# Three 16-element vectors: loaded as rows and spread over the partitions by a matmul with ones, instead of loaded spread

## The chip, the cores and the metric

The kernel runs on one core of a Trainium2 chip. The metric is the device time of one execution in microseconds (us); the median of three runs of the kernel before is 1518.44 us (1517.57 to 1518.94). TensorE (PE) multiplies, VectorE (DVE) and ScalarE (ACT) work elementwise, GpSimd (POOL) does little here, and the sixteen DMA engines move data. SyncE (SP) issues nearly all transfers on one queue (q1 in the profile), POOL issues a few on another (q0), ACT two at the start (q10). All queues are served by the same sixteen DMA engines.

## What is computed

One decoder block over 1024 tokens of width 1024 in float32: RMSNorm, one input projection, a Mamba-2 mixer beside a retention mixer, an output projection, a SwiGLU feed-forward, a final RMSNorm. The change touches only how three vectors with one value for each of the 16 Mamba heads reach the chip:

```python
dt = jax.nn.softplus(dt_raw.astype(jnp.float32) + dt_bias.astype(jnp.float32))
a = -jnp.exp(a_log.astype(jnp.float32)).reshape(SSD_GROUPS, SSD_HPG)
a_cs = jnp.cumsum(dt_c * a, axis=2)
...
d = d_skip.astype(jnp.float32).reshape(SSD_GROUPS, SSD_HPG, 1)
y = y_diag + y_off + x_c.astype(jnp.float32) * d
```

`dt_bias`, `a_log` and `d_skip` are (1, 16) each, 64 bytes.

## The kernel before

Every float32 product is made from three matmuls: each operand is split into a rounded part and a remainder (ACT copies, line 248; DVE subtracts, line 249). The program is a list of steps. A block is one strip of up to 512 columns of a weight with 8 or more steps, usually one for each 128 rows of the weight; a step runs 12 matmuls of up to 512 columns. `advance` runs ahead of the steps: it issues the weight loads (`load`, line 238, on SP, into a ring of five buffers `wr`) and the splits (`divide`, lines 248 and 249). `at(i, f)` hangs other work behind step i.

The program's start is written by hand. SP's queue holds, in order: a tile of x (`x0`, 512 KB), four weight tiles of 256 KB (below: weight tiles 0 to 3), the next tile of x (`x1`, 512 KB), then weight tiles 4 to 7, and after them narrower weight tiles, `x2`, `x3` and the constants `kcB`. ACT's queue holds the identity (64 KB) and one small load. The first block, `v0`, keeps all its eight weight tiles, split, in `m0` to `m7`. Its 8 steps are run token tile by token tile: 12 matmuls with weight tiles 0 to 3 for token tile 0, then `x1` is transposed (`turn`, 8 transposes, line 163), 12 matmuls with weight tiles 4 to 7 for token tile 0, 12 with tiles 0 to 3 for token tile 1, and so on. `turn(t)` also has ACT (line 1177) and DVE (line 1178) scale the transposed tile and split it into `h0` to `h7`. ACT works strictly in the program's order, in which the splits of weight tiles 4 to 7 alternate with pieces of `h`.

The names that the change touches:
- `hb` (128 x 32) holds `dt_bias` and `-exp(a_log)`, the same on each of the 128 partitions. `dcol` (128 x 8) holds `d_skip`, the even heads on partitions 0 to 63 and the odd ones on 64 to 127. `hb` is first read by the step that makes dt (line 510, at 57.05 us), `dcol` by the Mamba output (line 664, from 206.3 us).
- `load_small`, called while the start is laid out, issues the loads of `kcB` (SP) and of `dcol` and `hb` (POOL). `partition_broadcast` makes a source that is read again for each partition; for `dcol` the source is also read with a stride of two elements.
- `use_small` and `make_cols(False)` are called together from `late_small`, which hangs behind step 12. `make_cols` transposes the other small vectors (`rows`) on PE and copies them to `cols` by ACT.
- `bank("M")` draws the next of three PSUM banks in turn; `mm` is a matmul kept in program order; `T(shape, "at")` draws the buffer named `at`, which the kernel uses again later.

Of the kernel before, what the change touches and what calls it, by code (L numbers as in the profile page):

```python
# [12 lines left out]
AF = mybir.ActivationFunctionType  # L13
# [4 lines left out]
P = 128  # L18
# [6 lines left out]
SH, SP_, SG = 16, 64, 2  # L25
# [40 lines left out]
def block_kernel(ctx: ExitStack, tc: tile.TileContext, x, norm1_w, w_in, conv_w, conv_b,  # L66
                 dt_bias, a_log, d_skip, ssd_norm_w, ret_norm_w, w_out, norm2_w, w_gate,
                 w_up, w_down, final_norm_w, consts, out):
    nc = tc.nc
# [9 lines left out]
    def T(shape, tag, dt=F32, bufs=1):  # L79
        uid[0] += 1  # L80
        return sb.tile(list(shape), dt, tag=tag, name=f"{tag}_{uid[0]}", bufs=bufs)

    def bank(tag):
        uid[0] += 1
        return psum.tile([P, 512], F32, tag=tag, name=f"{tag}_{uid[0]}", bufs={"L": 5, "M": 3}[tag])
# [5 lines left out]
    act = nc.scalar.activation  # L91
# [17 lines left out]
    hb = T([P, 2 * SH], "hb")  # L109
    dcol = T([P, 8], "dcol")  # L110
    ones = T([P, P], "ones")
    nc.vector.memset(ones, 1.0)

    def use_small():
        act(hb[:, SH:2 * SH], hb[:, SH:2 * SH], AF.Exp)
        ts(hb[:, SH:2 * SH], hb[:, SH:2 * SH], -1.0, None, op0=ALU.mult)

    def load_small():
        nc.sync.dma_start(kc, consts[:, P:])
        for j in range(2):  # L120
            nc.gpsimd.dma_start(dcol[64 * j:64 * j + 64, :],
                                d_skip[0].rearrange("(k j) -> j k", j=2)[j]
                                .partition_broadcast(64))
        for j, src in enumerate((dt_bias, a_log)):
            nc.gpsimd.dma_start(hb[:, j * SH:(j + 1) * SH], src[0].partition_broadcast(P))

    dtb = hb[:, 0:SH]
    aneg = hb[:, SH:2 * SH]
# [30 lines left out]
    def mm(o, a, b, start=True, stop=True, **kw):  # L159
        tc.keep_in_program_order(nc.tensor.matmul(o, a, b, start=start, stop=stop, **kw))  # L160
# [1024 lines left out]
    b = bank("M")  # L1185
# [10 lines left out]
    for t in (2, 3):  # L1196
        first_load(t)
    load_small()
    at(ROWS, first_rows)

    def late_small():

        with tc.issue_after(newest["act"]), tc.issue_after(newest["dve"]):
            use_small()
            make_cols(False)
# [78 lines left out]
```

## Time and profile before

| | |
|---|---|
| median of the runs | 1518.44 us |
| the profiled execution | 1518.63 us |
| its span in the trace | 1516.8 us |
| PE busy | 1493.7 us (98%) |
| DVE busy | 1015.4 us (67%) |
| ACT busy | 630.4 us (42%) |
| granted PE clock, mean | 0.995 |

The chain of waits goes back from the last instruction to what released it, step by step; PE has 95% of the span in it and DMA 3%. Granted clock 1.00 is 2.4 GHz, 0.50 is 1.2 GHz. In a timeline each row is start and length in us, engine, line, operation, what is written and read, count, and in brackets the idle time before it with what ended it. In the table of stretches each row has, for each engine, busy us and count of instructions, then the granted clock (PEclk), the DMA engines' mean busy share (1.00 is all sixteen busy) and GB/s. In a table of DMA queues each row has packets, MB and the time the packets took as a share of sixteen engines' time.

### The profile page before, as it was taken

How to read it: one execution, taken by the hardware profiler on the slowest of the kernel's cores; microseconds unless marked ns; L12 is line 12 of the kernel's file. 1: busy time of each engine (PE TensorE's matmuls, PEld its weight loads, DVE VectorE, ACT ScalarE, POOL GpSimd, SP SyncE). 2: the span in 40 equal slices, each digit the busy share in tenths (PEclk: the TensorE clock that was granted, in tenths of full speed). 3: DMA queues.
4: the chain of work that ended last, by engine and by line, in shares of the span. 5: the costliest groups of instructions: out<-in, count | busy, mean ns of one | idle time of the engine just before them, and what ended most of it. 6: DMA issues, size and time to landing. Idle time of an engine off the chain costs nothing.

```text
span 1516.8 us, 20817 instructions
## 1 busy us (share of the span) xinstructions
PE 1493.7 (98%) x7408; PEld 1222.5 (81%) x7408; DVE 1015.4 (67%) x2171; ACT 630.4 (42%) x1223; POOL 35.9 (2%) x67
## 2 busy tenths in 40 slices
PE   7999999999999999999999999999999999999997
PEld 5888878888789878878888788888888887888886
DVE  4587698767688896579645977666666666346345
ACT  5344457444355665334544532233323334334231
POOL 1011000000001000000000000000000000000000
PEclk8999999999999999999999999999999999999999
DMA  7433466463425558645534323222222328355331
GB/s 197 137 92 98 113 208 187 126 236 111 133 71 152 165 181 268 222 140 175 190 116 131 111 82 107 84 77 84 84 82 79 97 96 309 116 187 182 125 118 63
DMA packets 141481, 209.73 MB, mean 138 GB/s; under 512 B 11236, under 2 KB 71488, under 8 KB 141376
## 3 DMA queue, kind: packets, MB, share of 16 engines
q1 hardware_dynamic: 140208, 206.95, 43.7%
q0 software_dynamic: 432, 0.59, 0.6%
q8 instruction: 58, 0.95, 0.3%
q10 hardware_dynamic: 736, 0.86, 0.2%
q14 instruction: 47, 0.39, 0.1%
HBM read 167.39 MB, written 40.96 MB: 137 GB/s over the span
## 4 chain that ended last, share of the span: by engine, by line
PE 95%; DMA 3%; ACT 1%; DVE 1%; issue 0%; SPq 0%; ACTq 0%
PE L L160 76%; PE M L160 17%; PE M L163 2%; DMA m<-aD 1%; DMA wr<-in_w_in_dram 1%; DMA wr<-in_w_down_dram 0%; DMA qk<-aD 0%; DMA kc<-in_consts_dram 0%; ACT m L195 0%; SPq L1058 0%; DVE wp L249 0%; ACT x L449 0%; DVE m L196 0%; ACT wp L248 0%; DVE u L1020 0%
## 5 line engine op out<-in xcount | busy, mean ns | idle before, releaser
L249 DVE TENSOR_TENSOR wp<-wr,wp 128x512 fp32r<-128x512 f32 (+2 forms) x328 | 218.2, 666 | 226.6 <-ACT wp L248 223.6
L160 PE MATMUL L<-wp,m 128*128 128x512 f32 x1512 | 356.1, 395 | 0.5 <-DVE wp L249 0.3
L248 ACT ACTIVATE wp<-wr 128x512 fp32r<-128x512 f32 (+2 forms) x328 | 199.7, 609 | 361.2 <-PE L L160 303.2
L160 PEld LDWEIGHTS L<-wp,m 128*128 128x128 f32 x1512 | 282.3, 188 | 66.2 <-DVE wp L249 0.8
L160 PE MATMUL L<-h,wp 128*128 128x512 f32 x1104 | 266.5, 397 | 0.0
L160 PE MATMUL L<-wp,h 128*128 128x512 f32 (+2 forms) x1248 | 260.0, 365 | 0.0
L160 PEld LDWEIGHTS L<-h,wp 128*128 128x128 f32 x1104 | 205.4, 188 | 49.5 <-issue 1.0
L160 PEld LDWEIGHTS L<-wp,h 128*128 128x128 f32 x1248 | 215.3, 188 | 30.6 <-issue 5.1
L160 PE MATMUL L<-m,x 128*128 128x512 f32 x336 | 82.3, 393 | 0.0
L160 PE MATMUL L<-m,wp 128*128 128x512 f32 x312 | 77.0, 395 | 0.0
L160 PEld LDWEIGHTS L<-m,x 128*128 128x128 f32 x336 | 63.0, 188 | 14.8
L160 PEld LDWEIGHTS L<-m,wp 128*128 128x128 f32 x312 | 58.5, 188 | 14.2
L392 DVE SCALAR_TENSOR_TENSOR m<-m,cols,m 128x512 f32<-128x512 f32 x72 | 52.1, 745 | 3.6 <-ACT m L390 3.4
L160 PE MATMUL M<-m,wp 128*128 128x512 f32 x216 | 53.5, 396 | 0.0
L160 PE MATMUL L<-h,x 128*128 128x512 f32 x204 | 50.6, 396 | 0.5 <-DVE wr L1018 0.5
L160 PEld LDWEIGHTS M<-m,wp 128*128 128x128 f32 x216 | 40.5, 188 | 10.1 <-DVE wp L196 0.3
L1011 ACT ACTIVATE wr<-wr 128x512 f32<-128x512 f32 x33 | 20.9, 632 | 66.0 <-DVE wr L1009 64.9
L160 PE MATMUL M<-m,x 128*128 128x512 f32 x192 | 47.1, 394 | 0.0
L160 PEld LDWEIGHTS L<-h,x 128*128 128x128 f32 x204 | 38.1, 188 | 10.0 <-DVE wr L1018 1.0
L195 ACT ACTIVATE x<-x 128x512 fp32r<-128x512 f32 x27 | 17.0, 629 | 64.5 <-PE L L160 43.6
L196 DVE TENSOR_TENSOR m<-m 128x512 fp32r<-128x512 f32 x32 | 21.9, 691 | 32.6 <-ACT m L195 32.3
L160 PEld LDWEIGHTS M<-m,x 128*128 128x128 f32 x192 | 36.0, 188 | 8.6
(294 smaller groups left out, 1981.6 us busy)
## 6 DMA issues: line engine op xcount, KB each, us to landing
wr<-in_w_in_dram SPq DMA_DIRECT2D x144, 256.0 KB, 2.7
wr<-in_w_down_dram SPq DMA_DIRECT2D x88, 256.0 KB, 2.9
wr<-in_w_out_dram SPq DMA_DIRECT2D x64, 256.0 KB, 3.0
aD<-u SPq DMA_DIRECT2D x44, 256.0 KB, 2.0
x<-in_w_gate_dram SPq DMA_DIRECT2D x22, 512.0 KB, 3.9
x<-in_w_up_dram SPq DMA_DIRECT2D x22, 512.0 KB, 4.6
x<-in_x_dram SPq DMA_DIRECT2D x16, 512.0 KB, 4.1
m<-rD SPq DMA_DIRECT2D x16, 512.0 KB, 4.2
```

Source lines behind the costliest of these rows:

```text
L160: tc.keep_in_program_order(nc.tensor.matmul(o, a, b, start=start, stop=stop, **kw))
L163: tc.keep_in_program_order(nc.tensor.transpose(o, a, ident))
L195: a = act(pair[:, 0], src, AF.Copy).ins
L196: d = tt(pair[:, 1], src, pair[:, 0].bitcast(F32), op=ALU.subtract).ins
L248: newest["act"] = act(pair[:, 0, :n], raw[:, :n], AF.Copy).ins
L249: newest["dve"] = tt(pair[:, 1, :n], raw[:, :n], pair[:, 0, :n].bitcast(F32), op=ALU.subtract).ins
L392: stt(dst, u[:, q:q + TH], w[q], dst, op0=ALU.mult, op1=ALU.add)
L1011: act(t, g, AF.Tanh, scale=0.5)
```

## The change

`load_small` now loads only `kcB`. Three loads of 16 elements each bring `dt_bias`, `a_log` and `d_skip` into one row `small` on one partition; they are issued on POOL's queue ahead of the memset of `halo`. `use_small` makes one matmul with a row of ones (one partition, 128 columns) as the stationary operand and `small` (one partition, 48 columns) as the moving one, which leaves the 48 values on all 128 partitions of a PSUM bank. From there ACT copies `dt_bias`, takes the exponential of `a_log`, and copies the even and odd elements of `d_skip` to the two halves of `dcol`; DVE negates as before.

```diff
+    small = T([1, 3 * SH], "at")
+    for j, src in enumerate((dt_bias, a_log, d_skip)):
+        nc.gpsimd.dma_start(small[:, j * SH:(j + 1) * SH], src)
+
     def use_small():
-        act(hb[:, SH:2 * SH], hb[:, SH:2 * SH], AF.Exp)
+
+        b = bank("M")
+        mm(b[:, :3 * SH], ones[:1, :], small)
+        act(hb[:, :SH], b[:, :SH], AF.Copy)
+        act(hb[:, SH:2 * SH], b[:, SH:2 * SH], AF.Exp)
         ts(hb[:, SH:2 * SH], hb[:, SH:2 * SH], -1.0, None, op0=ALU.mult)
+        d = b[:, 2 * SH:3 * SH].rearrange("p (k j) -> p j k", j=2)
+        for j in range(2):
+            act(dcol[64 * j:64 * j + 64, :], d[64 * j:64 * j + 64, j, :], AF.Copy)
 
     def load_small():
         nc.sync.dma_start(kc, consts[:, P:])
-        for j in range(2):
-            nc.gpsimd.dma_start(dcol[64 * j:64 * j + 64, :],
-                                d_skip[0].rearrange("(k j) -> j k", j=2)[j]
-                                .partition_broadcast(64))
-        for j, src in enumerate((dt_bias, a_log)):
-            nc.gpsimd.dma_start(hb[:, j * SH:(j + 1) * SH], src[0].partition_broadcast(P))
```

POOL's order at the program's start, before: two loads for `dcol` (64 partitions, 8 runs of one element each) and two for `hb` stand behind the memset.

```order
L105 DMA rows_66<-in_ssd_norm_w_dram 8x128
L140 MEMSET halo_79 128x36
L121 DMA dcol_75<-in_d_skip_dram 64x8x1 x2
L125 DMA hb_74<-in_dt_bias_dram 128x16
L125 DMA hb_74<-in_a_log_dram 128x16
```

And of the changed kernel at the same place:

```order
L105 DMA rows_66<-in_ssd_norm_w_dram 8x128
L116 DMA at_78<-in_dt_bias_dram 1x16x1
L116 DMA at_78<-in_a_log_dram 1x16x1
L116 DMA at_78<-in_d_skip_dram 1x16x1
L145 MEMSET halo_83 128x36
```

Four loads have become three; the elements written went from 1024 single ones and 256 runs of 16 to 48 single ones (the last number of a shape is the run).

ACT's order around step 12, before: the exponential stands between two splits of weight tiles (line 248), the copies to `cols` (line 137) behind them.

```order
L248 ACTIVATE wp_89_573<-wr_85_537 128x272
L115 ACTIVATE hb_5_74<-hb_5_74 128x16
L248 ACTIVATE wp_92_597<-wr_86_554 128x272
L137 ACTIVATE cols_8_78<-M_90_590 128x8
L137 ACTIVATE cols_8_78<-M_90_590 128x68
L137 ACTIVATE cols_8_78<-M_90_590 128x8
```

And of the changed kernel (line 253 is the split, line 142 the copies to `cols`):

```order
L253 ACTIVATE wp_90_573<-wr_85_537 128x272
L253 ACTIVATE wp_94_602<-wr_87_554 128x272
L122 ACTIVATE hb_5_74<-M_91_588 128x16
L123 ACTIVATE hb_5_74<-M_91_588 128x16
L127 ACTIVATE dcol_6_75<-M_91_588 64x8 x2
L142 ACTIVATE cols_9_82<-M_92_595 128x8
L142 ACTIVATE cols_9_82<-M_92_595 128x68
```

The one instruction has become four, which read PSUM and stand behind the split and directly ahead of the copies to `cols`.

## Rows read from the trace of the kernel before

**Rows 1.** Chain of waits, 0 to 60 us: start, length in us, what.
```profile
5.03 13.78 DMA wr<-in_w_in_dram
...
19.77 1.65 PE L L160 x3
21.42 1.71 PE M L163 x8
23.12 6.46 PE L L160 x24
29.58 0.87 PE M L163 x8
30.45 5.49 PE L L160 x24
...
52.59 0.07 PE M L135
```

**Rows 2.** Timeline of ACT, 5 to 28 us.
```profile
8.65 0.71 ACT L1177 ACTIVATE h<-M,cols 128x128 fp32r<-128x128 f32 x2
18.83 0.63 ACT L248 ACTIVATE m<-wr 128x512 fp32r<-128x512 f32 x1 [9.47 <-DMA wr<-in_w_in_dram]
...
19.62 0.62 ACT L248 ACTIVATE m<-wr 128x512 fp32r<-128x512 f32 x1
...
22.31 0.62 ACT L1177 ACTIVATE h<-M,cols 128x128 fp32r<-128x128 f32 x2 [0.51 <-PE M L163]
...
27.74 0.39 ACT L1177 ACTIVATE h<-M,cols 128x128 fp32r<-128x128 f32 x1
```

**Rows 3.** Stretches of the start: PE, PEld, DVE, ACT, POOL busy; PEclk, DMA share, GB/s.
```profile
0.00:8.00 8.00, 6.35 (x30) 5.33 (x30) 1.71 (x4) 3.48 (x7) 5.58 (x14) 1.00 0.80 264
8.00:15.00 7.00, 2.10 (x6) 0.97 (x6) 2.07 (x5) 1.36 (x4) 0.00 (x0) 0.99 1.10 48
...
10.40:19.80 9.40, 0.03 (x1) 0.03 (x1) 0.31 (x1) 0.97 (x3) 0.00 (x0) 0.74 0.79 137
19.80:25.00 5.20, 5.20 (x16) 4.33 (x17) 3.93 (x10) 4.46 (x14) 0.00 (x0) 0.50 0.90 315
```

**Rows 4.** DMA queues, 8 to 15 us: packets, MB, share of 16 engines.
```profile
q0 software_dynamic: 52, 0.01, 97.0%
q1 hardware_dynamic: 161, 0.33, 12.6%
```

**Rows 5.** DMA queues, 15 to 19 us, POOL's queue.
```profile
q0 software_dynamic: 80, 0.02, 2.0%
```

**Rows 6.** DMA issues: count, KB each, median us from issue to landing.
```profile
dcol<-in_d_skip_dram POOLq DMA_DIRECT2D x2, 2.0 KB, 11.5
rows<-in_conv_w_dram POOLq DMA_DIRECT2D x1, 24.0 KB, 4.7
...
hb<-in_dt_bias_dram POOLq DMA_DIRECT2D x1, 8.0 KB, 13.5
```

**Rows 7.** Timeline of the issues on SP and POOL, 0 to 30 us.
```profile
5.03 10.48 SPq L238 DMA_DIRECT2D wr<-in_w_in_dram  x5
...
5.51 0.59 POOL L125 DMA_DIRECT2D hb<-in_dt_bias_dram  x1
```

**Rows 8.** Timeline of ACT and PE, 50 to 56 us.
```profile
51.44 0.20 ACT L115 ACTIVATE hb<-hb 128x16 f32<-128x16 f32 x1
...
52.42 0.24 PE L135 MATMUL M<-kc,rows 84*128 84x84 f32 x1
...
52.62 0.43 ACT L248 ACTIVATE wp<-wr 128x272 fp32r<-128x272 f32 x1 [0.98 <-PE L L160]
52.96 0.34 ACT L137 ACTIVATE cols<-M 128x8 f32<-128x8 f32 x3
...
54.26 0.64 ACT L248 ACTIVATE wp<-wr 128x512 fp32r<-128x512 f32 x1 [0.95 <-PE L L160]
```

**Rows 9.** Groups of ACT by line: busy us, mean ns, idle before.
```profile
L137 ACT ACT_TABLE_LOAD x1 | 1.3, 1283 | 1.8 <-issue 1.8
```

## The prediction

> **What bounds the kernel now.** I read the chain of waits first. Nearly the whole span in it is PE, so a change counts if it shortens the time in which PE has nothing to do, or in which its clock is low. The largest such time is at the start: a load of a weight tile takes 13.78 us from its issue at 5.03 us and is followed by a split on ACT at 18.83, and only then does PE go on [rows 1, 2]. The timeline of ACT shows the same from its side: it ends a piece of h at 9.36 (8.65 + 0.71), then waits 9.47 us for a weight tile [rows 2]. This is weight tile 4, the fifth on SP's queue. The stretches show what this costs twice: from 10.4 to 19.8 PE has 0.03 us of work, the granted clock is 0.74 on average there, and from 19.8 to 25.0 it is 0.50, which is 1.2 GHz, while PE is busy all the time [rows 3].
>
> Next I asked what the DMA engines did meanwhile. Up to 8 us they moved 264 GB/s, from 8 to 15 us 48 GB/s, at a DMA share of 1.10 [rows 3]: busy, but moving nothing. The queues tell who held them: from 8 to 15 us POOL's queue has 52 packets and 0.01 MB at 97.0% of sixteen engines' time, SP's queue 0.33 MB at 12.6% [rows 4]. POOL's loads at that time are the two of dcol and the two of hb. The two of dcol are 2 KB each and land after 11.5 us in the median, against 4.7 us for the twelve times larger load of conv weights just ahead on the same queue [rows 6]. The loads of hb, 16 KB together, are issued from 5.51 us on and land 13.5 us later, about 19 us, and from 15 to 19 us POOL's queue moves 0.02 MB at only 2.0% [rows 5 to 7]. So it is dcol, not hb, that holds the engines: 97.0% of 16 engines for 7 us is 108.6 us of engine time for 1024 separate elements of four bytes, 0.106 us each. The hb packets, whose runs are 16 elements long, cost 1.3 us of engine time in all.
>
> The Trainium skill, DMA: Bandwidth & Descriptors, section Rules for kernel authors, says that a strided last dimension lowers to one descriptor for each element. The trace agrees, with 0.106 us for each element here.
>
> **The change part by part.** *The loads.* The four loads go, and with them the 108.6 us of engine time. Three loads come, each listed as 16 runs of one element, so they are still element by element: 48 elements instead of 1024. At 0.106 us each that is 5.1 us of engine time, 0.3 us if spread over sixteen engines. The bounds are nothing (the packets of hb, 80 of which with their neighbours took 1.3 us) and one whole dcol packet for each of the three loads on each engine; I take 0.3, because the number of elements is what the 97.0% follows. They follow the same five loads on POOL's queue as dcol's did, and nothing waits for them until step 12.
>
> The Trainium skill, same page, section Why a DMA increments its semaphore by 16, says that software can split a contiguous row so that it goes over sixteen engines; the listing's 1x16x1 fits. By this splitting the sum is 0.3 us; without it, with a row of 64 bytes as one run, it would be nothing.
>
> *When weight tile 4 comes now.* Ahead of its last byte on the queues are 0.11 MB of small things, x0 and x1 (1.05 MB) and five weight tiles (1.31 MB), 2.47 MB. By 8.0 us 2.11 MB had moved (264 GB/s by 8 us) [rows 3]. The other 0.36 MB takes 1.1 us at the 315 GB/s of the stretch from 19.8 to 25.0, 1.4 us at 264: it lands at 9.1 to 9.4, with the new elements at 9.4 to 9.7. ACT is free for it at 9.36. I take 9.6, so the split that started at 18.83 starts **9.2 us earlier**. Bounds: 9.47 (no wait at all) and 8.5: tiles 5 to 7 follow each other in 0.83 to 0.99 us (262 KB at those rates) where ACT takes one each 0.79 us (18.83 to 19.62) [rows 2], which can lose another 0.1 to 0.6. SP issued four of them late because the issues themselves were held, five issues in 10.48 us [rows 7]; with the engines free I expect them as soon as their buffers are.
>
> *The clock.* Up to the stall the granted clock is 1.00 with PE busy 6.35 of 8 us [rows 3]; it falls after PE had been idle for some microseconds, and without that idleness I expect it to stay at 2.4 GHz. Before, the way from 19.77 to 29.58 was 3 matmuls in 1.65, 8 transposes in 1.71 and 24 matmuls in 6.46 us, together 9.82 [rows 1]. At full clock 24 matmuls take 5.49 (0.229 each) and 8 transposes 0.87 [rows 1]; the same work is 27 x 0.229 + 0.87 = 7.05. That is 2.77 us less, if ACT and DVE keep up. What is late next is ACT: it evacuates token tile 1 without a gap from 22.31 to 28.13 [rows 2]. Without PE's slow transposes it begins this when the fourth split is done, 3.0 us after the first one starts (3 x 0.79 + 0.62) instead of 3.5. PE needs the fourth piece about 7.5 us after the first split, ACT and DVE give it some 0.3 us later than that. I take **2.4 us**, bounds 1.5 (ACT's squares of x get in the way further) and 2.77.
>
> *The tail of the shift.* After 30.45 the chain is PE without a break [rows 1], and the weight tiles and x2, x3 behind on SP's queue move forward with it, since they wait for buffers that are free earlier, or for the queue. I count the shift whole to the end.
>
> *Step 12.* PE gets one more small matmul, next to the transposition of the small vectors, which takes 0.24 us of PE's time and 0.07 on the chain [rows 1, 8]. Bounds 0.07 and 0.24, I take **0.1**. Its three loads are long done. ACT gets four small instructions where it had one of 0.20 us; like their neighbours they are 0.11 (three in 0.34) to 0.20 each, so 0.45 to 0.8 us, directly ahead of the copies to cols. Queued behind them are these copies and the split at 54.26. Before, ACT ended the copies at 53.30 and then waited 0.95 us for PE to free a split buffer [rows 8]: this wait hides them. Without that cover they would cost up to 0.8 us. Copies and exponentials alternate in both kernels, and the whole execution has one table load [rows 9], so none is added. DVE's negation comes one split later; hb is needed at 57 us, dcol at 206. One more draw of a PSUM bank makes each next draw wait for the one three draws back, which is long free there: nothing.
>
> **The sum**, against the profiled execution's own 1518.63 us, 0.2 above the median: - 9.2 - 2.4 + 0.1 = - 11.5, **1507.1 us**. With the bounds: - 9.47 - 2.77 + 0.07 gives 1506.5, - 8.5 - 1.5 + 0.24 gives 1508.9.
>
> **The rivals.** *Packets cost by their number, not by their elements, and the new loads are slower (slower than before).* The two loads of dcol, if each is one packet on each of sixteen engines, are 32 packets of 3.4 us (108.6 / 32). If a packet of one element were held as long, three loads would hold each engine 10.2 us instead of 6.8, and weight tile 4 would come 3.4 us later than now: 1522.0. It decides from 2.3 us for such a packet (6.8 / 3). For it: 1x16x1 is again one element at a time. Against it: 52 packets with 0.01 MB took 108.6 us, 80 with 0.02 MB 1.3 us [rows 4, 5], so it isn't the number.
>
> *They cost in between.* A short packet may be held for part of a latency. At the mean of the 52 packets, 2.1 us (108.6 / 52), three hold an engine 6.3 us, 6.0 more than in my sum: 1513.1; at 0.5 us each, 1.5 us, it is 1508.3. Middle of it: 1510.5. For it: nothing in the trace shows a one-element packet of data. Against: transfers ahead of them on the queue pass in 4.7 us with little engine time. The Trainium skill, DMA: Bandwidth & Descriptors, section Anatomy of one DMA, gives a fixed cost of about 2.0 us for each DMA, most of it the write's receipt; if that were engine time, this rival's upper end would be the result, an estimate of 1512.8 from that page.
>
> *The clock falls all the same*, because PE in this phase waits often in small pieces, so only the wait is won: 1518.63 - 9.2 + 0.1 = 1509.5. Against it: those small waits stood at clock 1.00 before 10 us.
>
> *The change doesn't do what it says*: something else, such as POOL's loads as such, holds the engines: 1518.7, no change. Against it: rows 5.
>
> **How the numbers follow.** A measurement of this kernel can tell about 0.2%, 3.0 us, from no change. My forecast of 1507.1 (1506.4 to 1508.9) has 0.78; in-between packets 0.10; the clock lost 0.05; no change 0.03; slower by packets 0.04. The first three are faster by over 0.2%: 0.93. The range holds my forecast with its bounds and the runs' own scatter (0.9 us), the lost clock and the nearer half of the in-between case: 1505.6 to 1510.4.
>
> **What would show it.** In the changed kernel's trace ACT's wait for a weight tile near 9.4 us should be under 0.5 us, POOL's queue should be under 5% of the engines' time from 8 to 15 us, PE's granted clock should be 1.00 throughout the first 30 us, and the 24 matmuls after the transposes of x1 should take about 5.5 to 5.9 us. Around the 12th step ACT should still wait for PE before the split that follows the copies to cols. I am wrong if POOL's queue still holds the engines for microseconds, if weight tiles 5 to 7 come late for another reason (issues on SP), or if PE waits on ACT for more than 1 us in the evacuation of token tile 1.

## The result

The changed kernel takes 1507.95 us in the median of four runs (1506.98 to 1508.86), the kernel before 1518.43 us (1517.57 to 1518.94): ratio 0.9929, 95% interval 0.9918 to 0.9941, 10.5 us less. 1507.1 us was forecast, 1505.6 to 1510.4 as the range.

The chain of waits of the changed kernel from 0 to 60 us answers to [rows 1]. Lines of the file have moved by 5: 165, 168, 253 and 1182 are what 160, 163, 248 and 1177 were.

```profile
5.24 5.07 DMA wr<-in_w_in_dram
...
10.33 0.63 ACT m L253
...
11.27 1.24 PE L L165 x3
12.51 0.87 PE M L168 x8
13.38 5.47 PE L L165 x24
18.85 0.88 PE M L168 x8
...
41.84 0.35 PE M L165 x2
42.19 0.22 PE M L140
42.41 3.08 PE L L165 x24
```

The load of weight tile 4 now lands 5.07 us after its issue instead of 13.78. The split that started at 18.83 starts at 10.33, 8.50 us earlier. From there to the end of the 24 matmuls behind the second turn (29.58 before, 18.85 now) another 2.23 us are won. At step 12 the two small matmuls have 0.57 us of the chain where one had 0.07.

The stretches answer to [rows 3], POOL's and SP's queues from 8 to 15 us to [rows 4], the timeline of ACT to [rows 2]:

```profile
8.00:15.00 7.00, 5.85 (x26) 3.89 (x26) 6.06 (x16) 6.31 (x18) 0.00 (x0) 1.00 0.96 294
10.40:19.80 9.40, 8.79 (x47) 6.97 (x46) 6.32 (x17) 9.40 (x31) 0.00 (x0) 1.00 0.93 309
19.80:25.00 5.20, 5.20 (x24) 4.27 (x23) 4.35 (x20) 3.74 (x14) 0.00 (x0) 1.00 0.90 287
```

```profile
q1 hardware_dynamic: 1046, 2.06, 94.8%
q0 software_dynamic: 96, 0.00, 0.8%
```

```profile
10.33 0.63 ACT L253 ACTIVATE m<-wr 128x512 fp32r<-128x512 f32 x1 [0.69 <-DMA wr<-in_w_in_dram]
```

PE has 8.79 us of work from 10.4 to 19.8 where it had 0.03, at a granted clock of 1.00; the engines move 294 GB/s from 8 to 15 us where they moved 48; POOL's queue takes 0.8% of their time instead of 97.0%, SP's 94.8% instead of 12.6%. ACT still waits for weight tile 4, but 0.69 us instead of 9.47.

### The profile page after: what moved, and what is told of

Same layout as the page of the kernel before. It is cut to its first block, busy times and chain, and to the rows that moved or that the text cites. A ratio compares the mean times of both kernels' runs of the same rounds, so it can differ in the third digit from the quotient of the medians.

```text
span 1507.1 us, 20824 instructions
## 1 busy us (share of the span) xinstructions
PE 1492.6 (99%) x7410; PEld 1220.5 (81%) x7410; DVE 1014.5 (67%) x2171; ACT 631.1 (42%) x1226; POOL 36.6 (2%) x66
## 4 chain that ended last, share of the span: by engine, by line
PE 93%; DMA 4%; DVE 1%; ACT 1%; issue 1%; SPq 0%; ACTq 0%; DVEq 0%
PE L L165 74%; PE M L165 17%; PE M L168 2%; DMA m<-aD 2%; DMA wr<-in_w_down_dram 1%; DVE wp L254 1%; ACT m L200 0%; DMA wr<-in_w_in_dram 0%; DMA kc<-in_consts_dram 0%; DMA qk<-aD 0%; DVE m L201 0%; SPq L243 0%; ACT wp L253 0%; ACT x L454 0%; DVE u L1025 0%
## 5 line engine op out<-in xcount | busy, mean ns | idle before, releaser
L165 PEld LDWEIGHTS M<-m,wp 128*128 128x128 f32 x216 | 40.4, 188 | 10.4 <-DVE wp L201 0.4
```

## The experiments

Ten kernels were run. In each, "split of tile 4" is ACT's split of weight tile 4, which ends the stall.

### Which of the loads held the engines

`d_row_only`: only d_skip as a row, dt_bias and a_log spread as before. The edit is against the changed kernel, and `use_small` follows it.

```diff
-    small = T([1, 3 * SH], "at")
-    for j, src in enumerate((dt_bias, a_log, d_skip)):
-        nc.gpsimd.dma_start(small[:, j * SH:(j + 1) * SH], src)
+    small = T([1, SH], "at")
+    nc.gpsimd.dma_start(small, d_skip)
...
     def load_small():
         nc.sync.dma_start(kc, consts[:, P:])
+        for j, src in enumerate((dt_bias, a_log)):
+            nc.gpsimd.dma_start(hb[:, j * SH:(j + 1) * SH], src[0].partition_broadcast(P))
```

> The changed kernel with only d_skip loaded as a row and spread by the matmul; dt_bias and a_log are loaded spread over 128 partitions as before. Theory (the two strided loads of dcol hold the DMA engines, the loads of hb don't): the wait of ACT for weight tile 4 stays under 1 us, its split starts near 10.3 us, time about 1508 us. Rival (POOL's spreading loads as such hold them): part of the stall comes back, split after 12 us, time 1510 to 1518 us.

`hb_rows_only`: the reverse, with the two strided loads of dcol as before.

```diff
-    small = T([1, 3 * SH], "at")
-    for j, src in enumerate((dt_bias, a_log, d_skip)):
+    small = T([1, 2 * SH], "at")
+    for j, src in enumerate((dt_bias, a_log)):
...
     def load_small():
         nc.sync.dma_start(kc, consts[:, P:])
+        for j in range(2):
+            nc.gpsimd.dma_start(dcol[64 * j:64 * j + 64, :],
+                                d_skip[0].rearrange("(k j) -> j k", j=2)[j]
+                                .partition_broadcast(64))
```

> The changed kernel with only dt_bias and a_log as rows; d_skip is loaded by the two strided, spreading loads as before. Theory: the stall stays whole, the split of weight tile 4 starts near 18.8 us, POOL's queue has over 90% of the engines from 8 to 15 us, time 1518 to 1519 us. Rival (hb): split before 12 us, time under 1511 us.

Measured: `d_row_only` 1508.96 us, ratio to the kernel before 0.9941 (0.9923 to 0.9959); `hb_rows_only` 1518.19 us, 1.0001 (0.9991 to 1.0011). ACT's waits in `d_row_only`, then in `hb_rows_only`:

```profile
11.37 0.63 ACT L252 ACTIVATE m<-wr 128x512 fp32r<-128x512 f32 x1 [1.86 <-DMA wr<-in_w_in_dram]
```

```profile
14.00 0.63 ACT L253 ACTIVATE m<-wr 128x512 fp32r<-128x512 f32 x1 [4.60 <-DMA wr<-in_w_in_dram]
...
19.77 0.63 ACT L253 ACTIVATE m<-wr 128x512 fp32r<-128x512 f32 x1 [4.88 <-DMA wr<-in_w_in_dram]
```

POOL's queue from 8 to 15 us in `d_row_only`, then in `hb_rows_only`:

```profile
q0 software_dynamic: 93, 0.02, 13.3%
```

```profile
q0 software_dynamic: 113, 0.00, 94.5%
```

With dcol's loads the whole stall is there, only cut in two (4.60 us before the split of tile 4, 4.88 before that of tile 5), where one at 18.8 was expected; without them it is gone. So dcol it is. But the loads of hb are not quite free: with them the split of tile 4 comes at 11.37, behind a wait of 1.86 us where under 1 was expected; without them it comes at 10.01 to 10.33 (in `late_spread`, `changed_again` and the changed kernel). POOL's queue has 13.3% of the engines instead of 0.8%.

### What of dcol's loads is slow

`d_contiguous`: the same partitions and the same count of elements, in runs of eight.

```diff
-                                d_skip[0].rearrange("(k j) -> j k", j=2)[j]
-                                .partition_broadcast(64))
+                                d_skip[0, 8 * j:8 * j + 8].partition_broadcast(64))
```

> The kernel before, with the two loads of dcol reading eight neighbouring elements for each partition instead of every second one (so the heads' d values stand in another order; the output differs for that). Same 1024 elements, same 64 partitions twice, but runs of 32 bytes. Theory (single four-byte elements are slow): the stall is gone, split of weight tile 4 near 10.3 us, time about 1507.5 us. Rival (repeating the source for 64 partitions is slow): stall whole, 1518 us.

Measured: 1509.35 us, ratio 0.9943 (0.9925 to 0.9962). ACT and POOL's queue from 8 to 15 us:

```profile
10.69 0.63 ACT L247 ACTIVATE m<-wr 128x512 fp32r<-128x512 f32 x1 [1.20 <-DMA wr<-in_w_in_dram]
```

```profile
q0 software_dynamic: 126, 0.02, 19.8%
```

The stall is gone with the stride. Repeating a source for 64 partitions isn't what is slow. Waits of 1.20 us for tile 4 and 0.84 us for tile 5 (split at 12.41) are left; the loads of hb, which cost about 1 us in `d_row_only`, are in this kernel too.

`d_by_columns`: 16 loads of 64 partitions by one element; `d_by_quarters`: 4 loads of 64 by four. Both keep the 1024 single elements.

```diff
         for j in range(2):
-            nc.gpsimd.dma_start(dcol[64 * j:64 * j + 64, :],
-                                d_skip[0].rearrange("(k j) -> j k", j=2)[j]
-                                .partition_broadcast(64))
+            for k in range(8):
+                nc.gpsimd.dma_start(dcol[64 * j:64 * j + 64, k:k + 1],
+                                    d_skip[0, 2 * k + j:2 * k + j + 1].partition_broadcast(64))
```

> The kernel before, with dcol loaded by 16 loads of 64 partitions x 1 element instead of 2 loads of 64 x 8. Again 1024 single elements, but each of an engine's successive elements goes to another partition, and an engine gets 4 of a load instead of 32. Theory A (a single element costs its engine 0.106 us wherever it goes): POOL's queue again has some 108 us of engine time before 20 us (60% of the engines or more from 8 to 15 us), split of weight tile 4 after 14 us, time 1513 to 1520 us. Theory B (only elements that follow each other in one partition, or many in one packet, are slow): POOL's queue under 15% from 8 to 15 us, split before 11.5 us, time near 1509 us.

```diff
         for j in range(2):
-            nc.gpsimd.dma_start(dcol[64 * j:64 * j + 64, :],
-                                d_skip[0].rearrange("(k j) -> j k", j=2)[j]
-                                .partition_broadcast(64))
+            for k in (0, 4):
+                nc.gpsimd.dma_start(dcol[64 * j:64 * j + 64, k:k + 4],
+                                    d_skip[0].rearrange("(k j) -> j k", j=2)[j, k:k + 4]
+                                    .partition_broadcast(64))
```

> The kernel before, with dcol loaded by 4 loads of 64 partitions x 4 single elements (stride two in the source, as before) instead of 2 loads of 64 x 8. An engine gets 16 single elements of a load, 4 after each other in one partition. If following one another in one partition is what is slow: each engine's share of a load takes some 1.5 us, POOL's queue has over 50% of the engines from 8 to 15 us, split of weight tile 4 after 13 us, time 1512 to 1519 us. If it takes the 32 of the original: POOL's queue under 15%, split before 12 us, time near 1509 us.

Measured: `d_by_columns` 1509.27 us, 0.9937 (0.9915 to 0.9960); `d_by_quarters` 1516.46 us, 0.9989 (0.9977 to 1.0000). The queues from 8 to 15 us and ACT's wait, of `d_by_columns`:

```profile
q1 hardware_dynamic: 851, 1.67, 66.5%
q0 software_dynamic: 282, 0.00, 2.5%
```

```profile
11.60 0.63 ACT L248 ACTIVATE m<-wr 128x512 fp32r<-128x512 f32 x1 [1.93 <-DMA wr<-in_w_in_dram]
```

and of `d_by_quarters`:

```profile
q0 software_dynamic: 89, 0.00, 50.1%
q1 hardware_dynamic: 174, 0.35, 14.0%
```

```profile
18.88 0.63 ACT L249 ACTIVATE m<-wr 128x512 fp32r<-128x512 f32 x1 [9.10 <-DMA wr<-in_w_in_dram]
```

From 8 to 15 us 282 packets cost 2.8 us of engine time (2.5% of 16 x 7) in the one, 89 packets 56.1 us in the other. In `d_by_columns` the loads run on behind it, since POOL issues the last of the 16 at 15.10; from 8 to 22 us POOL's queue takes 2.7%, 6.0 us of engine time with hb's loads in it, where the kernel before has 49.1% and `d_by_quarters` 31.4%. So a price for each single element, which my sum used, is wrong: theory A of the first expectation falls. The stall comes with four or eight single elements that follow each other in one partition, and not with one for each partition. That this following is the cause, and not another difference of the two (16 elements of a load for each engine against 4, a stride in the source against none), fits but isn't separated.

The time of POOL's packets isn't all that such loads cost. In `d_by_columns` they take 2.5%, yet SP's queue has 66.5% and moves 1.67 MB, where the changed kernel has 94.8% and 2.06 MB; the split of tile 4 came at 11.60, 0.1 us behind the 11.5 that I had set for theory B. In `d_by_quarters` SP's queue has only 14.0% while POOL's leaves it half of the engines' time. What holds SP's loads back there stays open.

### The clock

`warm_stall`: the kernel before, with matmuls that were to keep PE busy in the stall.

```diff
+                    if self.first == 0 and k == 0 and kk == 3:
+                        for _ in range(20):
+                            mm(self.ps[1][:, :P], ones, ones)
                     self.three(self.ps[j], j, kk, self.pair[kk])
```

> The kernel before, with 20 extra matmuls of ones on PE (about 8.8 us at the rate of the nine at the start) ahead of the matmul that waits through the stall; their result is overwritten. The stall itself stays. Theory (2.2 us of the gain are the clock that no longer falls): granted clock 1.00 all along, the split of tile 4 still near 18.8 us, time 1516.2 us. Rival (all of the gain is the wait): time 1518.4 us or more.

Measured: 1521.79 us, 1.0028 (1.0019 to 1.0038), some 4 us more than the kernel before. PE's timeline tells that it was no test:

```profile
10.65 4.63 PE L160 MATMUL L<-ones 128*128 128x128 f32 x40
20.87 1.65 PE L160 MATMUL L<-m,h 128*128 128x512 f32 x3 [5.59 <-ACT h L1180]
...
29.40 0.96 PE L160 MATMUL L<-m,h 128*128 128x512 f32 x3 [0.45 <-ACT h L1180]
```

Each of these float32 matmuls stands as two instructions in the trace, called passes here. The 20 matmuls are 40 passes of 0.116 us, half of the time that I had counted, so PE was idle for 5.59 us all the same and its clock fell (0.57 on average from 19.8 to 25.0 us). Besides, ACT's squares of x now stood ahead of pieces of h, for which PE then waited.

`warm_stall_2` has 40 such matmuls, and holds the squares and the first splits of the second block behind pieces of h (`BEHIND` lists for each square the piece it follows).

```diff
-        with tc.issue_after(newest["act"]):
-            for b in range(2):
+        for b in range(2):
+            with tc.issue_after(newest["act"]), tc.issue_after(newest[BEHIND[t][b]]):
...
+            pin = {8: (1, 7), 9: (2, 0), 10: (2, 6), 11: (3, 7)}.get(divided[0])
...
+                        for _ in range(40):
+                            mm(self.ps[1][:, :P], ones, ones)
```

> The kernel before with 40 extra matmuls of ones (80 passes of 0.116 us, 9.3 us) in the stall, and ACT's order held near that of the kernel before. The stall stays. Theory (2.2 us of the gain are the clock): granted clock 1.00 up to 30 us, split of tile 4 near 18.8 to 20 us as before, and from that split on PE needs 2.2 us less to the end of token tile 1; time 1516 us where the kernel before has 1518. Rival (the clock cost nothing, ACT sets the pace): time as before or up to 0.3 us more.

Measured: 1517.31 us, 0.9990 (0.9981 to 0.9998), 1.3 us less than the median of the kernel before beside it (1518.60; 0.3 to 2.9 us by the interval). Its stretches and its chain:

```profile
10.40:19.80 9.40, 8.91 (x80) 8.72 (x79) 0.24 (x1) 0.91 (x3) 0.00 (x0) 1.00 0.79 132
19.80:25.00 5.20, 5.17 (x26) 4.09 (x27) 4.58 (x12) 4.56 (x13) 0.00 (x0) 1.00 0.97 335
```

```profile
18.89 0.63 ACT m L248
...
21.06 0.87 PE M L163 x8
21.94 5.70 PE L L160 x24
27.64 0.88 PE M L163 x8
```

The stall stands (split at 18.89), the clock is 1.00 throughout, and PE ends the 24 matmuls at 27.64 instead of 29.58, though ACT waited 0.5 us more for weight tile 7 in it. ACT's order is another here, too, but it can't have given these 2 us: in the kernel before, PE's timeline has no idle time in the 8 transposes and the 24 matmuls behind the stall, so ACT held up none of them:

```profile
21.21 1.91 PE L163 MATMUL M<-kc,x 128*128 128x128 f32 x8
22.77 6.80 PE L160 MATMUL L<-m,h 128*128 128x512 f32 x24
```

So about 2 us belong to the clock, as the traces of before and after say (2.23).

### Two ways to go on

`changed_again` is the changed kernel once more, run beside the other two and `warm_stall_2` to compare them with.

> The changed kernel once more, as the base for the other three on the same chip. Both theories: 1507 to 1509 us, split of weight tile 4 near 10.3 us.

`tile4_first` issues five weight tiles ahead of x1.

```diff
-    for k in range(4):
+    for k in range(5):
         A0.load(k)
-    issued[0] = 4
+    issued[0] = 5
```

> The changed kernel with weight tile 4 issued ahead of x1 instead of behind it. Theory (a load lands about 1.2 us after its last byte by the count of bytes, because the slowest of the sixteen engines ends it, and that is why tile 4 came at 10.3 instead of 9.6): with 0.5 MB less ahead of it, tile 4 is there before ACT wants it, its split starts near 9.6 us without a wait, and up to 0.7 us is won if tiles 5 to 7 follow in time: 1507.2 to 1507.9 us if the changed kernel has 1507.9. Rival (SP's issues set the pace, or x1 comes late now): no gain, or PE waits for x1.

`late_spread` has no rows and no matmul; POOL's loads wait for x2.

```diff
+        nc.gpsimd.tensor_copy(dall[:, :1], xin[2][:, :1])
+        for j in range(2):
+            nc.gpsimd.tensor_copy(hb[:, j * SH:j * SH + 1], xin[2][:, :1])
+        nc.gpsimd.dma_start(dall, d_skip[0].partition_broadcast(P))
+        for j, src in enumerate((dt_bias, a_log)):
+            nc.gpsimd.dma_start(hb[:, j * SH:(j + 1) * SH], src[0].partition_broadcast(P))
...
+            nc.gpsimd.tensor_copy(dcol[64 * j:64 * j + 64, :], d[64 * j:64 * j + 64, j, :])
```

> No matmul and no rows: all three vectors loaded spread over 128 partitions in runs of 16 elements, but POOL issues these loads only after x2 has landed (it copies an element of x2 into each buffer first); POOL then makes dcol from the spread d_skip by two copies. Theory (the stall came only from dcol's single elements, the loads of hb cost about 1 us at the start and nothing later, the matmul costs 0.35 us of PE at step 12): split of tile 4 near 10.2 us, no step of 0.35 us at step 12, time 0.3 to 0.5 us under the changed kernel. Rival (spread loads slow whatever they meet): a wait on weight tiles or x3 of over 1 us appears after 15 us, time over the changed kernel.

Measured: `changed_again` 1508.39 us, 0.9932 (0.9919 to 0.9944), with the split of tile 4 at 10.18; `tile4_first` 1508.43 us, 0.9933 (0.9919 to 0.9946); `late_spread` 1507.49 us, 0.9928 (0.9915 to 0.9940). ACT and PE in `tile4_first`:

```profile
9.07 0.63 ACT L253 ACTIVATE m<-wr 128x512 fp32r<-128x512 f32 x1
...
10.79 0.63 ACT L253 ACTIVATE m<-wr 128x512 fp32r<-128x512 f32 x1 [0.31 <-DMA wr<-in_w_in_dram]
...
12.23 0.63 ACT L253 ACTIVATE m<-wr 128x512 fp32r<-128x512 f32 x1 [0.56 <-DMA wr<-in_w_in_dram]
```

```profile
11.73 0.96 PE L165 MATMUL L<-m,h 128*128 128x512 f32 x3 [0.75 <-ACT h L1182]
```

Tile 4 is the fifth split, at 9.07: it waited for no load, as the theory had it. But tiles 5 and 6, now behind x1, were waited for 0.31 and 0.56 us, and the piece of h that PE waits for stands behind the split of tile 5 here, so PE went on at 11.73 (11.27 in the changed kernel). The wait moved to the next tiles, and nothing was won. In `late_spread` the chain at step 12 and POOL's queue from 15 to 25 us, after that the split of tile 4:

```profile
41.51 0.07 PE M L140
```

```profile
q0 software_dynamic: 96, 0.02, 10.1%
```

```profile
10.01 0.63 ACT L253 ACTIVATE m<-wr 128x512 fp32r<-128x512 f32 x1 [0.66 <-DMA wr<-in_w_in_dram]
```

The transposition at step 12 has 0.07 us again, and the spread loads, two of which took 13.3% of the engines in `d_row_only`, take 10.1% here, three of them, while the chain is PE alone from 18.53 us to step 12. By the traces step 12 takes 0.5 us less of the chain than in the changed kernel (0.07 against 0.57); the 0.9 us between the medians can't be told from no difference, since both intervals overlap nearly whole.

## Why the prediction was right, step by step

*That dcol holds the engines* was right, by `d_row_only` and `hb_rows_only`. That hb is free was not: its loads cost about 1.0 us (11.37 against 10.33) where the queues are full; the 2.0% that I read from 15 to 19 us [rows 5] was at a time when all engines together moved 192 GB/s, against 294 from 8 to 15 us in the changed kernel. Nor is 0.106 us the price of an element, as `d_by_columns` shows.

*When tile 4 comes*: 8.50 us earlier, where 9.2 was taken, and just at the lower bound of 8.5. The bound was met by luck: it stood for tiles 5 to 7 coming late, and their splits followed at 11.12, 11.89 and 12.68 without a wait. The term mis-sized is the landing at 9.4 to 9.7; it landed at 10.31. The bytes went as I had counted, as the stretches of the changed kernel up to 9.10 and 10.33 us show:

```profile
0.00:9.10 9.10, 6.80 (x32) 5.54 (x32) 2.53 (x6) 4.31 (x9) 4.59 (x13) 1.00 0.78 272
0.00:10.33 10.33, 8.03 (x36) 6.20 (x36) 3.76 (x9) 4.85 (x11) 4.59 (x13) 1.00 0.81 280
```

2.47 MB had moved by 9.1 us (272 x 9.1 = 2475 KB), and the tile landed 1.2 us later. At that landing 2.89 MB had moved (280 x 10.33), so by the count some 0.4 MB of what stands behind the tile had run before it was there. The kernel before had shown such a lag: weight tile 2 was complete by count (1.42 MB) at 6.25 us, and ACT, which waited for it, got it at 7.34:

```profile
0.00:6.25 6.25, 4.87 (x26) 4.69 (x27) 0.17 (x1) 1.95 (x4) 5.19 (x14) 1.00 0.71 227
```

```profile
7.34 0.63 ACT L248 ACTIVATE m<-wr 128x512 fp32r<-128x512 f32 x1 [0.22 <-DMA wr<-in_w_in_dram]
```

The lag is the sum's missing term; what it consists of stays open. The 0.3 us for the new elements wasn't needed (0.8% of the engines is 0.9 us of engine time, 0.06 us for each engine).

*The clock*: 2.23 us against 2.4, the mechanism shown by `warm_stall_2`. What was lost to full speed lies elsewhere than I had put it. The 24 matmuls took 5.47 us and waited for nothing; the first three took 1.24 instead of 0.69, 0.55 us more. Their last matmul needs a remainder that DVE makes behind that of tile 4:

```profile
11.60 0.78 DVE L1183 SCALAR_TENSOR_TENSOR h<-M,cols,h 128x128 fp32r<-128x128 f32 x2
```

In `tile4_first` the same three took 0.96 us, with the first of them behind a wait of 0.75 us as well; so I put about half of the 0.55 to DVE and the rest to PE's start after its idle time, which no run separates.

*The tail*: behind step 12 the changed kernel is 10.25 us ahead (the 24 matmuls there end at 45.49 instead of 55.74), and the two spans differ by 9.7 us (1516.8 and 1507.1). The runs of the changed kernel alone lie 1.9 us apart, so the shift was kept to the end as far as they can tell.

*Step 12* was undersized: 0.50 us (0.57 against 0.07) where 0.1 was taken and 0.24 was the upper bound. I had priced the new matmul by the transposition beside it, which is one pass. The timelines of PE and of its weight loads (PEld) in the changed kernel show two passes of the new one:

```profile
41.77 0.29 PEld L165 LDWEIGHTS M<-at,ones 1*128 1x128 f32 x2 [0.15 <-issue]
41.77 0.42 PE L165 MATMUL M<-at,ones 1*128 1x48 f32 x2
```

The matmul has 0.35 us of the chain, and hardly less with fewer columns: 0.32 with 16 in `d_row_only`, 0.33 with 32 in `hb_rows_only`:

```profile
42.87 0.32 PE M L164 x2
50.22 0.33 PE M L165 x2
```

So the price hardly follows the columns; that it is the two passes and their weight loads (0.29 us by the row above) fits this. The transposition behind it has 0.22 us instead of 0.07, in these two kernels as well; why stays open. The sign of the two passes was in the kernel before: nine matmuls of ones at its start stand as 18 in the trace. ACT's part of step 12 went as forecast:

```profile
42.23 0.18 ACT L122 ACTIVATE hb<-M 128x16 f32<-128x16 f32 x1
...
42.37 0.35 ACT L127 ACTIVATE dcol<-M 64x8 f32<-64x8 f32 x2
42.73 0.36 ACT L142 ACTIVATE cols<-M 128x8 f32<-128x8 f32 x3
44.01 0.64 ACT L253 ACTIVATE wp<-wr 128x512 fp32r<-128x512 f32 x1 [0.91 <-PE L L165]
```

The four take 0.50 us, and the wait for PE behind the copies is still 0.91 us.

*The rivals.* A one-element packet that holds its engine for 0.5 us or more, and with it the slower case, is excluded by the 96 packets at 0.8%. The clock didn't fall, and the time did. Three figures of the prediction are slightly off and change nothing: ACT's work from 22.31 has a gap of 0.23 us, the low end of the forecast is 1506.5 and not 1506.4, and the middle of 1508.3 and 1513.1 is 1510.7 and not 1510.5. Of the signs that I had named, ACT's wait for tile 4 was 0.69 us and not under 0.5; the others came as written (POOL's queue 0.8%, the clock 1.00 over the first 30 us, the 24 matmuls 5.47 us, ACT's wait behind the copies). The terms as measured make - 8.50 - 2.23 + 0.50 = - 10.2 from 1518.63, 1508.4, against the 1508.85 of the profiled execution and the median of 1507.95.

## What to carry to other kernels

Where the DMA engines are busy and move nothing, split their time by queue: here 4 KB in single elements, eight for each partition, took 97.0% of the sixteen engines' time from 8 to 15 us and held up the loads of the other queue. The split shows who holds the engines, not all that it costs: in `d_by_columns` POOL's queue had only 2.5%, and SP's was slower all the same. A few values that all partitions need can be read as rows into one partition and spread by a matmul, or loaded spread, in runs of several elements, at a time when nobody waits for a transfer. And a stall that idles PE is to be priced twice, by the wait and by the low clock behind it; here 8.50 and 2.23 us were won.

## What was not expected of the hardware

- Single elements loaded one for each partition took 282 packets and 2.8 us of engine time from 8 to 15 us; loaded four to a partition, 89 packets and 56.1 us in the same stretch. The price isn't one for an element, and SP's queue was slower beside both.
- With the queue full, a weight tile landed 1.1 and 1.2 us after the count of bytes said that it was complete (weight tile 2 before, weight tile 4 after the change).
- A float32 matmul of one row by 48 columns had 0.35 us of the chain (0.32 with 16 columns), and the transposition of 84 rows behind it 0.22, where that had 0.07 in the kernel before.
